# Mixer of a hybrid layer: decay on ScalarE alone, the group norm's factor in steps of their own, and three smaller moves

## The chip, the core and the metric

One core of a Trainium2 chip runs the whole layer in one launch. The metric is device time in microseconds (us), the median of several runs. The engines are TensorE (PE in the rows; PEld its weight loads), VectorE (DVE), ScalarE (ACT), GpSimd (POOL) and SyncE (SP), which issues most loads. Each works through its own queue of instructions in order and waits on semaphores of the others.

## The reference

One decoder layer with 512 tokens of width 1024 in float32: a SwiGLU feed-forward network (FFN1), a mixer, a second one (FFN2), a gated embedding and a final norm. The change touches the mixer alone. Cut to what matters there:

```python
n = rmsnorm(h, mix_norm)
u, v, z, xbc, dt_raw = split(n @ w_in)
ya = rmsnorm(chunked_spatial_gating(gelu(u), gelu(v), ...), gm_out_norm)
xs, b, c = split(silu(causal_depthwise_conv(xbc)))
dt = softplus(dt_raw + dt_bias); a = -exp(a_log)
a_cs = cumsum(dt * a)                               # in chunks of 128 tokens
decay = exp(a_cs[l] - a_cs[s]) for s <= l, else 0   # per head and chunk
y = ((c b^T) * decay) @ (xs * dt) + c @ previous_states * exp(a_cs) + xs * d_skip
y = y * silu(z)
y = y * rsqrt(mean over each of 2 groups (y*y) + eps) * norm_g
h = h + concat(ya, y) @ w_out
```

There are 16 heads of 64 in two groups, a state of 128, and four chunks of 128 tokens.

## The kernel before

Activations lie with features on the 128 partitions and 512 tokens along a row, eight tiles to 1024 features. A float32 product is made of three matmul passes over a high and a low part (L215, L216, L217: high by high, high by low, low by high). A weight tile of 128x1024 is loaded by SyncE (`raw`), cast to its high part on ScalarE (`whi`, L185), and its low part is the difference, made on VectorE (`wlo`, L186); each of the three has three buffers. In a z unit the third matmul is the first that reads `wlo`.

The feed-forward stages stand in an order written out by hand. The mixer's does not: a scheduler places its instructions by the order of the code, by its model of costs and by when buffers come free, and each engine's queue is the result.

The mixer begins with the product for dt (L943 to L954; eight tiles of the normed input, each with a high and a low part), the B and C convolutions and eight convolution tiles `xs`. Then comes the **scan loop** over eight pairs of heads j. A round has these steps:

- `project(13 + j)`, the z unit, 24 matmuls of 512 columns;
- for group 1, states (L1076, L1081, L1082) and `by_token` (transposes L1063, xdt L1065 on VectorE, its scaled copy L1069 on POOL);
- `rows_of`: for the pair after next, ScalarE issues DMAs that spread a head's cumulative sum from DRAM over all partitions (L1091), and in `decayed` two for the grown row (L1109);
- `decayed`: per head, POOL subtracts the column of sums (L1101), VectorE takes the minimum with zero (L1104), ScalarE the exponential (L1105), VectorE multiplies by the masked c b^T (L1106);
- `ssd`: 16 mask products (L1122) and the state products (L1127) on TensorE, then L1131 and L1132 on VectorE and L1133 on POOL add them to y;
- `gated`: z times r/2 (L1141), tanh (L1142), L1143, and y times that on POOL (L1144), whose square goes into the sum of its group's norm (L263 for a group's first tile, L266 and L267 for the next three).

Group 0 is done after pair 3, group 1 after pair 7. The group norm's factor needs four sums over partitions on TensorE (L276), a root in eleven tiny VectorE steps (L233 to L238), a tile of diagonals (L295), a product that spreads it over all partitions (L306), and a copy to SBUF (L312). `finish_group` then multiplies four y tiles (L1150) and splits each in a high part on ScalarE (L199) and a low part on POOL (L200). In the code of before the sums and root of group 0 are called at the first of the eight units of the w_v product, the other steps at the third; group 1's at the fourth and at the sixth.

After w_v come the gating (`mix`, between the u units, with sums for a norm in `gn`, whose additions L267 run on POOL) and the output product, which reads the split y.

Of the kernel before, what the change touches and what calls it, by code (L numbers as in the profile page):

```python
# [26 lines left out]
AF = mybir.ActivationFunctionType  # L27
ALU = mybir.AluOpType

P = 128  # L30
T = 512
NC = T // P
D = 1024
ND = D // P
# [7 lines left out]
D_ORDER = tuple(d + i for d in range(NP) for i in (0, NP))  # L42
# [21 lines left out]
GROUPS = 2  # L64
# [19 lines left out]
def layer_kernel(ctx: ExitStack, tc: tile.TileContext, a: dict, out: bass.AP):  # L84
    nc = tc.nc
# [73 lines left out]
    ps = sm_ps()  # L159
# [11 lines left out]
    class Unit:  # L171
# [11 lines left out]
        def split(self, c0, c1):  # L183
            c = slice(c0, c1)
            nc.scalar.copy(self.hi[:, c], self.raw[:, c])  # L185
            nc.vector.tensor_tensor(  # L186
                self.lo[:, c], self.raw[:, c], self.hi[:, c].bitcast(F32), ALU.subtract
            )
# [759 lines left out]
        both[:, :, :HEADS].bitcast(F32), ALU.subtract,  # L948
    )
    ps = mm_ps()  # L950
    for k in range(ND):
        for i in range(2):
            nc.tensor.matmul(
                ps, both[:, k, :], x[k][i], start=k + i == 0, stop=k + i == ND  # L954
            )
    dt_raw = tmp()
    nc.vector.tensor_copy(dt_raw[: 2 * HEADS], ps[: 2 * HEADS])
# [16 lines left out]
    def chunk(t, c):  # L974
        return t[:, c * P : (c + 1) * P]
# [17 lines left out]
    def hc(t):  # L993
        return t.rearrange("p (h c) -> p h c", c=NC)
# [100 lines left out]
    def decayed(j, ms):  # L1095

        g = j // 4
        for i, m in enumerate(ms):
            hd = 2 * j + i
            m3 = m.rearrange("p (c l) -> p c l", c=NC)  # L1100
            nc.gpsimd.tensor_tensor(  # L1101
                m3, m3, hc(acs)[:, hd, :].unsqueeze(2).to_broadcast([P, NC, P]), ALU.subtract
            )
            nc.vector.tensor_scalar(m, m, 0.0, None, ALU.min)  # L1104
            nc.scalar.activation(m, m, AF.Exp)  # L1105
            nc.vector.tensor_tensor(m, m, cb[g], ALU.mult)  # L1106
        grow = sb("u")
        for i in range(2):
            nc.scalar.dma_start(  # L1109
                grow[i * HD : (i + 1) * HD, :],  # L1110
                cs_dram[1, 2 * j + i : 2 * j + i + 1, :].partition_broadcast(HD),
            )
        return ms, grow
# [30 lines left out]
        nc.gpsimd.tensor_tensor(xs[j], xs[j], z, ALU.mult)  # L1144
        group_norm[j // 4].add(xs[j])

    def finish_group(g, tok):
        rg = Norm.on_all(tok)
        for j in range(4 * g, 4 * g + 4):
            nc.vector.scalar_tensor_tensor(  # L1150
                xs[j], xs[j], col("ssm_norm", j), rg, ALU.mult, ALU.mult
            )
            yb.append(split(xs[j], "yb"))

    xs = []
    for i in range(ND):
# [51 lines left out]
    for half in range(2):  # L1208
        ps = [mm_ps() for _ in range(NC)]
        for u in range(4):  # L1210
            whi, wlo = weights(w_v[half, u], 1024)
            if half == 0:
                if u == 0:
                    group_tok = [group_norm[0].per_token(D // GROUPS)]
                elif u == 2:
                    finish_group(0, group_tok[0])
                elif u == 3:
                    group_tok.append(group_norm[1].per_token(D // GROUPS))
            elif u == 1:
                finish_group(1, group_tok[1])  # L1220
            for c in range(NC):
                for i in range(2):
                    k = 2 * u + i
                    xhi, xlo = (chunk(t, c) for t in x[k])
                    w = slice(i * T, (i + 1) * T)
                    passes(ps[c], xhi, xlo, whi[:, w], wlo[:, w], k == 0, k == ND - 1)
        for c in range(NC):
            t = sb("ya")
            nc.scalar.activation(t, ps[c], AF.Gelu, scale=rtok[:, c : c + 1])
            v[c][half] = t  # L1230
# [33 lines left out]
        bias.append(b)  # L1264

    u = []
    gn = Norm()

    def mix(i):
        ps = sm_ps()  # L1270
# [277 lines left out]
```

## Time and profile before

| | us |
|---|---|
| median of 3 runs | 1109.0 |
| the runs | 1108.41, 1109.0, 1111.56 |
| the profiled execution, its own time | 1109.82 |
| its span in the trace | 1108.1 |
| TensorE busy | 1083.0 |
| VectorE busy | 792.1 |
| ScalarE busy | 494.5 |
| POOL busy | 172.6 |

The profiled execution is one of the program's; its span runs from its first to its last instruction, and 1.7 us lie around it. Its mean granted TensorE clock is 0.996 of full speed. The mixer's scan loop lies at about 445 to 518, the w_v product and the gating behind it. A row of the profile names the line, the engine, the operation and its tiles (output <- inputs) with their shapes. Where a row has a part in square brackets, that is how long the engine sat idle before it and what ended the wait.

### The profile page before, as it was taken

The page shows a single profiled execution, that of the slowest core. Times are in us where ns is not written, and L with a number is a line of the kernel's source. Part 1 is how long each engine was busy: PE and PEld are TensorE (multiplying, and loading weights), DVE is VectorE, ACT ScalarE, POOL GpSimd, SP SyncE. Part 2 cuts the span into 40 slices and gives each one's busy share as a digit, 9 for nine tenths or more (in the row PEclk, how much of TensorE's full clock was granted, in tenths as well). Part 3 has the DMA queues.
Part 4 walks back from the last instruction along what each step waited for, and adds up shares of the span by engine and source line. Part 5 has one row for each costly group of instructions (what it writes and reads, how often), then busy time and mean ns, then how long its engine had stood idle before and what let it go on. Part 6 is the DMA issues. An engine that isn't in the chain of part 4 may idle for free.

```text
span 1108.1 us, 16431 instructions
## 1 busy us (share of the span) xinstructions
PE 1083.0 (98%) x6631; PEld 952.7 (86%) x6631; DVE 792.1 (71%) x1072; ACT 494.5 (45%) x645; POOL 172.6 (16%) x155
## 2 busy tenths in 40 slices
PE   9889999999999999999999999999999999999997
PEld 6779999999998787777788888889999999999887
DVE  5887776766667688898775565768767766667766
ACT  6545444444345374433433343544444443434554
POOL 2001000000001201585421100000000000000311
PEclk9999999999999999999999999999999999999998
DMA  9767756566631223343422233477666666543412
GB/s 352 202 172 198 198 151 183 170 188 159 182 95 57 96 79 107 112 143 116 133 76 95 77 96 114 156 167 196 185 190 190 176 186 176 165 121 110 140 52 77
DMA packets 49036, 161.66 MB, mean 146 GB/s; under 512 B 5568, under 2 KB 5824, under 8 KB 48960
## 3 DMA queue, kind: packets, MB, share of 16 engines
q1 hardware_dynamic: 34128, 117.46, 30.9%
q0 software_dynamic: 9232, 33.56, 16.8%
q10 hardware_dynamic: 5600, 9.60, 2.8%
q8 instruction: 52, 0.85, 0.3%
q14 instruction: 24, 0.20, 0.1%
HBM read 156.33 MB, written 4.26 MB: 145 GB/s over the span
## 4 chain that ended last, share of the span: by engine, by line
PE 77%; DVE 12%; ACT 4%; issue 3%; POOL 2%; DMA 1%; SPq 0%; DVEq 0%; ACTq 0%; POOLq 0%
PE mm L598 18%; PE acc L598 14%; PE sm L216 8%; PE sm L217 8%; PE sm L215 8%; PE mm L215 4%; PE mm L216 4%; PE mm L217 4%; PE acc L215 3%; PE acc L216 3%; PE acc L217 3%; ACT whi L421 1%; DVE wlo L186 1%; DVE wlo L422 1%; DMA u<-cs_dram 1%
## 5 line engine op out<-in xcount | busy, mean ns | idle before, releaser
L598 PE MATMUL mm<-xfb,whi 128*128 128x256 f32 x960 | 166.4, 276 | 0.5 <-ACT whi L421 0.5
L422 DVE TENSOR_TENSOR wlo<-raw,whi 128x1024 fp32r<-128x1024 f32 x93 | 113.9, 1225 | 56.6 <-ACT whi L421 54.6
L598 PEld LDWEIGHTS mm<-xfb,whi 128*128 128x128 f32 x960 | 146.0, 188 | 2.3 <-ACT whi L421 0.7
L598 PE MATMUL mm<-xfb,wlo 128*128 128x256 f32 x480 | 132.8, 277 | 0.8 <-DVE wlo L422 0.8
L421 ACT CAST whi<-raw 128x1024 fp32r<-128x1024 f32 x93 | 97.3, 1047 | 78.4 <-issue 39.2
L217 PE MATMUL sm<-ghi,wlox 128*128 128x512 f32 x296 | 116.3, 393 | 0.0
L216 PE MATMUL sm<-glo,whix 128*128 128x512 f32 x296 | 115.8, 391 | 0.0
L215 PE MATMUL sm<-ghi,whix 128*128 128x512 f32 x296 | 115.2, 389 | 0.0
L598 PE MATMUL acc<-xfb,whi 128*128 128x256 f32 x640 | 111.2, 276 | 0.8 <-DVE g L730 0.8
L598 PEld LDWEIGHTS acc<-xfb,whi 128*128 128x128 f32 x640 | 97.8, 188 | 2.9 <-issue 1.4
L598 PE MATMUL acc<-xfb,wlo 128*128 128x256 f32 x320 | 88.7, 277 | 2.6 <-DVE wlo L422 2.6
L598 PEld LDWEIGHTS mm<-xfb,wlo 128*128 128x128 f32 x480 | 90.1, 188 | 1.0 <-DVE wlo L422 1.0
L422 DVE TENSOR_TENSOR wlox<-rawd,whix 128x1024 fp32r<-128x1024 f32 (+1 forms) x40 | 45.7, 1142 | 58.1 <-ACT whix L421 58.1
L422 DVE TENSOR_TENSOR wlo<-rawb,whi 128x1024 fp32r<-128x1024 f32 x52 | 63.6, 1223 | 21.3 <-ACT whi L421 21.3
L613 POOL DMA_DIRECT2D raw<-in_ffn_gu x20 | 17.3, 863 | 388.1 <-DVE h L790 121.2
L736 ACT ACTIVATE g<-g 128x512 f32<-128x512 f32 x40 | 25.3, 632 | 110.8 <-DVE g L735 110.8
L185 ACT CAST whi<-raw 128x1024 fp32r<-128x1024 f32 x44 | 45.7, 1043 | 59.7 <-PE mm L216 22.7
L186 DVE TENSOR_TENSOR wlo<-raw,whi 128x1024 fp32r<-128x1024 f32 x44 | 57.5, 1308 | 19.5 <-ACT whi L185 14.4
L790 DVE SCALAR_TENSOR_TENSOR h<-sm,h 128x512 f32<-128x512 f32 x96 | 63.5, 685 | 10.9 <-PE sm L217 10.3
L421 ACT CAST whi<-rawb 128x1024 fp32r<-128x1024 f32 x52 | 54.2, 1043 | 26.4 <-DVE rawb L608 19.7
L217 PEld LDWEIGHTS sm<-ghi,wlox 128*128 128x128 f32 x296 | 55.5, 188 | 11.7
L215 PEld LDWEIGHTS sm<-ghi,whix 128*128 128x128 f32 x296 | 55.6, 188 | 11.1 <-DVE h L790 0.4
(393 smaller groups left out, 2657.4 us busy)
## 6 DMA issues: line engine op xcount, KB each, us to landing
raw<-in_ffn_gu SPq DMA_DIRECT2D x56, 512.0 KB, 5.9
rawd<-in_ffn_down SPq DMA_DIRECT2D x40, 512.0 KB, 3.9
rawb<-in_ffn_gu SPq DMA_DIRECT2D x32, 512.0 KB, 5.1
raw<-in_ffn_gu POOLq DMA_DIRECT2D x30, 512.0 KB, 5.5
raw<-in_w_in SPq DMA_DIRECT2D x29, 512.0 KB, 3.6
s<-in_ffn_gu SPq DMA_DIRECT2D x20, 512.0 KB, 7.0
s<-in_ffn_gu POOLq DMA_DIRECT2D x20, 512.0 KB, 8.2
raw<-in_w_out SPq DMA_DIRECT2D x16, 512.0 KB, 3.5
```

The lines of the kernel that those rows point to most:

```text
L185: nc.scalar.copy(self.hi[:, c], self.raw[:, c])
L186: nc.vector.tensor_tensor(self.lo[:, c], self.raw[:, c], self.hi[:, c].bitcast(F32), ALU.subtract)
L215: nc.tensor.matmul(ps, whi, xhi, start=first, stop=False)
L216: nc.tensor.matmul(ps, whi, xlo, start=False, stop=False)
L217: nc.tensor.matmul(ps, wlo, xhi, start=False, stop=last)
L421: nc.scalar.copy(self.hi[:, :n], raw[:, :n])
L422: nc.vector.tensor_tensor(self.lo[:, :n], raw[:, :n], self.hi[:, :n].bitcast(F32), ALU.subtract)
L598: nc.tensor.matmul(o, wt[:, c], xt, start=fresh and p == m == n == 0, stop=last and n == 2, skip_group_check=True,)
L613: nc.gpsimd.dma_start(w21.raw, self.src[0], accum_op=ALU.add)
L736: nc.scalar.activation(t, t, AF.Silu)
L790: nc.vector.scalar_tensor_tensor(h[d], ps[d], 0.5, h[d], ALU.mult, ALU.add)
```

## The change

Five edits in the mixer. In `decayed`, POOL's subtraction and VectorE's minimum go. ScalarE makes four Relu instructions of 128x128 per head, one per chunk, each max(column - row, 0) with the column as bias, and the exponential is taken of minus that, so that the result is the same. The steps of the group norm's factor are functions of their own, called at separate units of w_v. The low parts of y, the split's difference, are made on VectorE, no longer on POOL. The gating norm `gn` adds its squares on VectorE. The product for dt takes its tiles in the order 0, 4, 1, 5, 2, 6, 3, 7 (`D_ORDER`), no longer 0 to 7; that is the order in which FFN1 finishes them.

```diff
--- before.py
+++ after.py
@@ -948,10 +948,10 @@
         both[:, :, :HEADS].bitcast(F32), ALU.subtract,
     )
     ps = mm_ps()
-    for k in range(ND):
+    for n, k in enumerate(D_ORDER):
         for i in range(2):
             nc.tensor.matmul(
-                ps, both[:, k, :], x[k][i], start=k + i == 0, stop=k + i == ND
+                ps, both[:, k, :], x[k][i], start=n + i == 0, stop=n + i == ND
             )
     dt_raw = tmp()
     nc.vector.tensor_copy(dt_raw[: 2 * HEADS], ps[: 2 * HEADS])
@@ -1097,12 +1097,12 @@
         g = j // 4
         for i, m in enumerate(ms):
             hd = 2 * j + i
-            m3 = m.rearrange("p (c l) -> p c l", c=NC)
-            nc.gpsimd.tensor_tensor(
-                m3, m3, hc(acs)[:, hd, :].unsqueeze(2).to_broadcast([P, NC, P]), ALU.subtract
-            )
-            nc.vector.tensor_scalar(m, m, 0.0, None, ALU.min)
-            nc.scalar.activation(m, m, AF.Exp)
+
+            for c in range(NC):
+                nc.scalar.activation(
+                    chunk(m, c), chunk(m, c), AF.Relu, scale=-1.0, bias=hc(acs)[:, hd, c : c + 1]
+                )
+            nc.scalar.activation(m, m, AF.Exp, scale=-1.0)
             nc.vector.tensor_tensor(m, m, cb[g], ALU.mult)
         grow = sb("u")
         for i in range(2):
@@ -1144,13 +1144,25 @@
         nc.gpsimd.tensor_tensor(xs[j], xs[j], z, ALU.mult)
         group_norm[j // 4].add(xs[j])
 
-    def finish_group(g, tok):
-        rg = Norm.on_all(tok)
+
+    group = [{}, {}]
+
+    def group_sums(g):
+        group[g]["ps"] = group_norm[g].sums()
+
+    def group_diagonals(g):
+        group[g]["diags"] = Norm.diagonals(Norm.of_sums(group[g]["ps"], D // GROUPS))
+
+    def group_spread(g):
+        group[g]["ps"] = Norm.spread(group[g]["diags"], group[g]["ps"])
+
+    def finish_group(g):
+        rg = Norm.kept(group[g]["ps"])
         for j in range(4 * g, 4 * g + 4):
             nc.vector.scalar_tensor_tensor(
                 xs[j], xs[j], col("ssm_norm", j), rg, ALU.mult, ALU.mult
             )
-            yb.append(split(xs[j], "yb"))
+            yb.append(split(xs[j], "yb", nc.vector))
 
     xs = []
     for i in range(ND):
@@ -1209,15 +1221,13 @@
         ps = [mm_ps() for _ in range(NC)]
         for u in range(4):
             whi, wlo = weights(w_v[half, u], 1024)
-            if half == 0:
-                if u == 0:
-                    group_tok = [group_norm[0].per_token(D // GROUPS)]
-                elif u == 2:
-                    finish_group(0, group_tok[0])
-                elif u == 3:
-                    group_tok.append(group_norm[1].per_token(D // GROUPS))
-            elif u == 1:
-                finish_group(1, group_tok[1])
+            for fn in {
+                (0, 0): (lambda: group_sums(0),), (0, 1): (lambda: group_diagonals(0),),
+                (0, 2): (lambda: group_spread(0),), (0, 3): (lambda: finish_group(0), lambda: group_sums(1)),
+                (1, 0): (lambda: group_diagonals(1),), (1, 1): (lambda: group_spread(1),),
+                (1, 2): (lambda: finish_group(1),),
+            }.get((half, u), ()):
+                fn()
             for c in range(NC):
                 for i in range(2):
                     k = 2 * u + i
@@ -1264,7 +1274,7 @@
         bias.append(b)
 
     u = []
-    gn = Norm()
+    gn = Norm(nc.vector)
 
     def mix(i):
         ps = sm_ps()
```

The scheduler places the instructions anew; behind the second edited line the line numbers are shifted (L1150 becomes L1162). Three places follow, as the queue of one engine in a row; the numbers behind the names count buffers, and what an instruction waits for stands in brackets.

VectorE, around the low part of z unit 6. First before, where `wlo_4725` is that low part, L1131 to L1132 the sums of pair 4, L1104 the minima of the masks of pair 6:

```order
L1141 SCALAR_TENSOR_TENSOR tmp_4690<-acc_4628,rall_3725 128x512 [waits DVE_49,PE_49]
L1131 SCALAR_TENSOR_TENSOR xs_4098<-xs_4098,vec_70,mm_4674 128x512 [waits PE_49]
L1132 TENSOR_TENSOR u_4596<-u_4596,sm_4675 128x384 [waits DMAHW5_49,DMAHW3_49,PE_49]
L1143 SCALAR_TENSOR_TENSOR tmp_4690<-tmp_4691,tmp_4690 128x512 [waits Activation_49]
L186 TENSOR_TENSOR wlo_4725<-raw_4723,whi_4724 128x1024
L1104 TENSOR_SCALAR u_4670<-u_4670 128x512 [waits DMAHW2_49,Pool_49]
L1104 TENSOR_SCALAR u_4672<-u_4672 128x512 [waits DMAHW3_49,Pool_49]
L1106 TENSOR_TENSOR u_4670<-u_4670,ya_4062 128x512 [waits Activation_49]
```

Then the same place after, where `wlo_4749` is that low part and L1131, L1132 the sums of pair 5:

```order
L1141 SCALAR_TENSOR_TENSOR tmp_4788<-acc_4722,rall_3725 128x512 [waits PE_49,Pool_49]
L1143 SCALAR_TENSOR_TENSOR tmp_4714<-tmp_4715,tmp_4714 128x512 [waits Activation_49]
L1131 SCALAR_TENSOR_TENSOR xs_4147<-xs_4147,vec_70,mm_4772 128x512 [waits PE_49]
L186 TENSOR_TENSOR wlo_4749<-raw_4747,whi_4748 128x1024 [waits DMAHW5_49,Activation_49]
L1132 TENSOR_TENSOR u_4691<-u_4691,sm_4773 128x384 [waits DMAHW1_49,DMAHW0_49]
L1106 TENSOR_TENSOR u_4694<-u_4694,ya_4062 128x512 [waits Activation_49]
L1106 TENSOR_TENSOR u_4696<-u_4696,ya_4062 128x512 [waits Activation_49]
```

The low part stood behind L1143 and now stands behind L1131 of the pair just ahead of the unit, and that waits for TensorE; the minima are gone from the row.

ScalarE, one round of the decay. First before, where `u_4516` and `u_4518` are the masks of one pair, L1109 and L1091 issue row copies:

```order
L1091 DMA u_4516<-cs_dram 128x512 [waits DMAHW1_49,PE_49]
L1091 DMA u_4518<-cs_dram 128x512 [waits DMAHW2_49,PE_49]
L1109 DMA u_4596<-cs_dram 64x512 [waits DMAHW3_49,PE_49]
L266 ACTIVATE tmp_4542<-xs_3985 128x512 [waits Activation_49,Pool_49]
L1109 DMA u_4596<-cs_dram 64x512 [waits DMAHW5_49]
L1091 DMA u_4599<-cs_dram 128x512 [waits DMAHW6_49,DVE_49]
L1091 DMA u_4601<-cs_dram 128x512 [waits DMAHW7_49,PE_49]
L1105 ACTIVATE u_4516<-u_4516 128x512 [waits DVE_49]
L1105 ACTIVATE u_4518<-u_4518 128x512 [waits DVE_49]
L1142 ACTIVATE tmp_4620<-tmp_4619 128x512
L1109 DMA u_4667<-cs_dram 64x512 [waits DMAHW0_49,PE_49]
L1109 DMA u_4667<-cs_dram 64x512 [waits DMAHW1_49]
```

Then after, where `u_4694` and `u_4696` are the rows of a pair, first issued and then read by Relu (L1102), and L185 is the cast of a z unit's weights:

```order
L1102 ACTIVATE u_4621<-u_4621,acs_3944 128x128 x3
L1109 DMA u_4691<-cs_dram 64x512 [waits PE_49]
L1105 ACTIVATE u_4621<-u_4621 128x512 [waits Activation_49]
L1109 DMA u_4691<-cs_dram 64x512
L1091 DMA u_4694<-cs_dram 128x512 [waits DMAHW2_49,PE_49]
L1091 DMA u_4696<-cs_dram 128x512 [waits DMAHW7_49,DMAHW3_49]
L1142 ACTIVATE tmp_4715<-tmp_4714 128x512 [waits DVE_49]
L185 CAST whi_4748<-raw_4747 128x1024
L1102 ACTIVATE u_4694<-u_4694,acs_3944 128x128 [waits DMAHW2_49]
L1102 ACTIVATE u_4694<-u_4694,acs_3944 128x128
L263 ACTIVATE ssum_4720<-xs_4098 128x512 [waits Pool_49]
L1102 ACTIVATE u_4694<-u_4694,acs_3944 128x128 x2
```

The exponential waited for VectorE's minimum; now a Relu waits for the DMA of its row, with one tanh and one cast between the DMA's issue and it, and the squares (L263) stand among the Relus.

VectorE, the diagonals of group 0 (L295), ahead of the first tile of y that is multiplied by the factor. First before, where L236 to L238 are the end of the root:

```order
L236 TENSOR_TENSOR nt_4904<-ny_4903 128x4 [waits DVE_49]
L237 SCALAR_TENSOR_TENSOR nt_4904<-nt_4904,nv_4902 128x4 [waits DVE_49]
L238 SCALAR_TENSOR_TENSOR rtok_4901<-nt_4904,ny_4903 128x4 [waits DVE_49]
L295 TENSOR_TENSOR tmp_4976<-ident_72,rtok_4901 128x512 [waits DVE_49,Pool_49]
L186 TENSOR_TENSOR wlo_5028<-raw_5026,whi_5027 128x1024 [waits DMAHW4_49,Activation_49]
L186 TENSOR_TENSOR wlo_5090<-raw_5088,whi_5089 128x1024 [waits DMAHW5_49,Activation_49]
L1150 SCALAR_TENSOR_TENSOR xs_3895<-xs_3895,vec_70,rall_4980 128x512 [waits Activation_49]
```

Then after, where `wlo_4959` to `wlo_5106` are low parts of w_v's units and L1141, L1143 the gate of the last pair:

```order
L1141 SCALAR_TENSOR_TENSOR tmp_4909<-mm_4868,rall_3725 128x512 [waits DVE_49,Pool_49]
L186 TENSOR_TENSOR wlo_4959<-raw_4957,whi_4958 128x1024 [waits DMAHW4_49,Activation_49]
L1143 SCALAR_TENSOR_TENSOR tmp_4909<-tmp_4910,tmp_4909 128x512 [waits Activation_49]
L186 TENSOR_TENSOR wlo_5006<-raw_5004,whi_5005 128x1024 [waits DMAHW1_49]
L295 TENSOR_TENSOR tmp_4978<-ident_72,rtok_4963 128x512 [waits DVE_49,Pool_49]
L186 TENSOR_TENSOR wlo_5037<-raw_5035,whi_5036 128x1024 [waits DMAHW4_49,Activation_49]
L186 TENSOR_TENSOR wlo_5106<-raw_5104,whi_5105 128x1024 [waits DMAHW5_49,Activation_49]
L1162 SCALAR_TENSOR_TENSOR xs_3895<-xs_3895,vec_70,rall_5041 128x512 [waits Activation_49]
```

The root's steps have left this place: they now stand ahead of the last pair's L1143, between the mask multiplications of the last pair. The diagonals stand between low parts of w_v's units. On TensorE the spread (L306) keeps its place, the same number of instructions from the start, while the sums of group 0 now stand ahead of z unit 7.

## Rows read from the trace of the kernel before

**Rows 1.** Page, part 1: busy us, share and instructions of each engine.

```profile
PE 1083.0 (98%) x6631; PEld 952.7 (86%) x6631; DVE 792.1 (71%) x1072; ACT 494.5 (45%) x645; POOL 172.6 (16%) x155
```

**Rows 2.** Whom TensorE waited for: us in total, times, longest.

```profile
PE mm L1122 <- DVE u L1106: 2.4, 3, 1.3
PE sm L306 <- DVE tmp L295: 2.3, 1, 2.3
PE mm L217 <- DVE wlo L186: 1.7, 1, 1.7
...
PE mm L953 <- DVE convin L961: 0.7, 1, 0.7
...
PE sm L276 <- POOL ssum L267: 0.3, 1, 0.3
```

**Rows 3.** Windows: length, busy PE, PEld, DVE, ACT, POOL; granted clock, DMA share, GB/s.

```profile
444.80:518.30 73.50, 69.38 (x393) 55.66 (x392) 66.83 (x79) 29.82 (x42) 47.80 (x34) 1.00 0.42 128
518.30:530.00 11.70, 11.70 (x58) 9.73 (x56) 8.27 (x16) 2.87 (x5) 6.74 (x6) 1.00 0.29 91
530.00:536.00 6.00, 3.71 (x9) 2.09 (x8) 5.22 (x9) 2.34 (x3) 1.22 (x1) 0.72 0.19 61
```

**Rows 4.** Timeline of TensorE at the spread: start, length, instruction, idle time before.

```profile
529.67 0.39 PE L216 MATMUL mm<-wlo,x 128*128 128x512 f32 x1
529.90 0.39 PE L217 MATMUL mm<-whi,x 128*128 128x512 f32 x1
532.58 2.04 PE L306 MATMUL sm<-tmp,ones 128*128 128x512 f32 x2 [2.29 <-DVE tmp L295]
...
535.70 0.45 PE L215 MATMUL mm<-whi,x 128*128 128x512 f32 x1
```

**Rows 5.** POOL's groups, 430 to 740: busy us, mean ns, idle before.

```profile
L1101 POOL TENSOR_TENSOR u<-u,acs 128x512 f32<-128x512 f32 x16 | 21.0, 1320 | 7.2 <-DMA u<-cs_dram 7.2
...
L1144 POOL TENSOR_TENSOR xs<-xs,tmp 128x512 f32<-128x512 f32 x8 | 13.6, 1698 | 3.2 <-DVE tmp L1143 2.8
...
L1069 POOL TENSOR_TENSOR u<-yb,toend 128x512 f32<-128x512 f32 x5 | 7.1, 1429 | 16.2 <-DVE yb L1065 16.2
```

**Rows 6.** VectorE's groups, 430 to 540, in the same columns.

```profile
L1104 DVE TENSOR_SCALAR u<-u 128x512 f32<-128x512 f32 x16 | 14.5, 923 | 0.9 <-POOL u L1101 0.9
...
L1143 DVE SCALAR_TENSOR_TENSOR tmp<-tmp,tmp 128x512 f32<-128x512 f32 x8 | 5.8, 727 | 0.0
...
L1131 DVE SCALAR_TENSOR_TENSOR xs<-xs,vec,mm 128x512 f32<-128x512 f32 x4 | 3.0, 739 | 0.0
```

**Rows 7.** Timeline of VectorE and POOL: two low parts, one beside POOL.

```profile
461.74 1.22 DVE L186 TENSOR_TENSOR wlo<-raw,whi 128x1024 fp32r<-128x1024 f32 x1
...
467.99 1.39 POOL L1133 TENSOR_TENSOR xs<-xs,u 128x384 f32<-128x384 f32 x1 [2.69 <-DVE u L1132]
...
468.43 2.03 DVE L186 TENSOR_TENSOR wlo<-raw,whi 128x1024 fp32r<-128x1024 f32 x1
```

**Rows 8.** ScalarE's groups with a column as operand, two widths.

```profile
L1374 ACT ACTIVATE tmp<-tmp,vec 128x512 f32<-128x512 f32 x5 | 3.6, 714 | 0.4 <-DVE tmp L1373 0.3
...
L1374 ACT ACTIVATE tmp<-tmp,vec 128x256 f32<-128x256 f32 x6 | 3.0, 496 | 2.1 <-DVE tmp L1373 2.1
```

**Rows 9.** Timeline of ScalarE: two instructions behind each other.

```profile
464.12 0.63 ACT L263 ACTIVATE ssum<-xs 128x512 f32<-128x512 f32 x1 [0.68 <-POOL xs L1144]
464.66 0.61 ACT L1105 ACTIVATE u<-u 128x512 f32<-128x512 f32 x1
```

**Rows 10.** Line L1091, the masks' row copies: from issue to landing.

```profile
DMA to landing us min/median/max: 3.0/3.5/5.2
```

**Rows 11.** Line L1109, row copies: ns per issue, min/median/max; first and last start.

```profile
L1109 ACTq DMA_DIRECT2D u<-cs_dram x16: 452/453/1456, 442.3 to 508.5; - x16
```

**Rows 12.** Timeline of TensorE: mask products of two pairs, five pairs apart.

```profile
461.72 1.58 PE L1122 MATMUL acc<-u,yb 128*64 128x128 f32 x16
...
507.78 1.58 PE L1122 MATMUL acc<-u,yb 128*64 128x128 f32 x16
```

## The prediction

> **What bounds the kernel now.** I read the busy times first: TensorE is busy 1083 of 1108 us [rows 1], so only its idle time, some 25 us, and a fallen clock can be won, and of these only what lies in the mixer. The list of who TensorE waited for [rows 2] names the places that the change can touch: the decay masks (L1122 behind L1106, 2.4 us in 3 waits), the spread of group 0's factor (L306 behind L295, 2.3), the low part of one z unit (L217 behind L186, 1.7), the last tile of dt's product (L953, 0.7) and the sums of a norm (L276 behind POOL's L267, 0.3). Then by stage [rows 3]: from the first z product to the end of the scan loop (444.8 to 518.3) TensorE is busy 69.4 of 73.5, idle 4.1; VectorE is busy 66.8 there, ScalarE 29.8, POOL 47.8. Around the spread (530 to 536) TensorE is busy 3.7 of 6.0 at a granted clock of 0.72. The single rows show it [rows 4]: the last matmul starts at 529.90, the spread at 532.58, and the matmuls after it come 0.43 apart up to 535.70, where full speed has them 0.23 apart (529.67 to 529.90).
>
> **The change part by part.**
>
> *The old waits of the scan loop, -4.1.* Per pair of heads two POOL subtractions (1.32 us each) and two VectorE minima (0.92) go: 16 x 1.32 = 21.0 us off POOL and 14.5 off VectorE [rows 5, 6]. VectorE also gets faster where POOL was running: a wlo subtraction takes 1.22 when POOL is still, and 2.03 when it starts 0.44 into a POOL instruction of 1.39 [rows 7], so VectorE is held until POOL has ended. With 66.8 - 14.5 = 52 us of work in 73.5, VectorE no longer trails the loop, and I drop all 4.1 us of the old idle time. Only the 0.5 of L1076 just ahead of 444.8 stays.
>
> *The work that ScalarE gets, hidden.* 64 Relu instructions of 128x128 with a column as bias are in no row. The same form takes 0.714 at 512 columns and 0.496 at 256 [rows 8]; the line through both gives 0.39 at 128, and since the next instruction starts about 0.09 before the end of one (464.12 to 464.66 for 0.63) [rows 9], 0.30 per step: 64 x 0.30 = 19 us. Bounds: a quarter of the 512 price, 0.18 (11 us), and the 256 price less the overlap, 0.41 (26 us). I take the line, as 128 lies nearest the 256 row on it. ScalarE would be busy 49 of 73.5 us. What is new is its queue order: the copies that bring pair j+2's rows are issued, then come one tanh, one weight cast and at once the Relus that wait for these copies. They land 3.5 us after issue (3.0 to 5.2) [rows 10]; behind the waiting Relus stand the next tanh and the next whi cast. A round is 3.5 landing + 8 x 0.30 Relu + 0.54 square + two exponentials 1.2 + three issues of 0.45 [rows 11] = 9.0 us. TensorE needs 46.1 us for five pairs (461.72 to 507.78) [rows 12], 9.2 each, and the masks are made a pair ahead. So I cost it at nothing; what decides this is in the third rival.
>
> [...]
>
> *New waits in the loop, +6.6.* The order on VectorE puts wlo of a z unit directly behind L1131 of the pair before it, and L1131 waits for that pair's last mask matmul on TensorE. TensorE goes straight on to the z unit, whose third matmul needs wlo. Chain: L1131, 0.74 long, next start 0.66 on [rows 6], wlo 1.22 free or 2.03 behind POOL [rows 7], hand-offs 0.1: 2.0 to 2.8. Two matmuls cover 0.23 + 0.39 = 0.6 [rows 4]. So 1.4 to 2.2 idle.
> - z unit 2: L1143 just ahead starts POOL's L1144, so nearly the upper end, 2.15.
> - z unit 6: L1143 runs while VectorE waits for TensorE, so half of POOL's time is over, 1.7.
> - z unit 7: group 0's sums now stand between, about 0.95 of small matmuls: 0.45 to 1.25, I take 0.7.
> - z unit 5: the pulled-up state products of later pairs cover it, 0.1.
> - z unit 3: a state product now stands after its second matmul and waits for L1069, which POOL does after L1144. From the transposes L1143 0.6, L1144 1.7, L1069 1.4 [rows 5, 6] with a start half a step late: 4.2, covered by the pair's products 2.3 and two matmuls 0.45: 1.5 (0.2 with POOL's fastest runs, 2.0 if also L1082 comes late).
> - pair 1, second head: L1132 now stands ahead of its L1106 and waits for that pair's state products; 0.5 + 0.7 less the first head's 0.8: 0.5 (0 to 1).
> Sum 6.6, between 3.5 and 8.7. Units 2 and 6 come near the one idle stretch (2.3) after which the clock fell; 1.7 (unit 6 of before) left it alone. I take no fall, and keep 1.6 for one in the range.
>
> *Group norm's factor, -3.9.* The spread keeps its place among TensorE's products; only VectorE's order moves. Group 0's sums come a z unit earlier, and the eleven tiny steps of the root and the diagonals no longer stand behind L1143 of the last pair; the diagonals stand behind the wlo of w_v's third unit, which is needed by the same matmuls anyway. By the rows, TensorE reaches the spread at about 530 [rows 4], while wlo is made some 4 us earlier. So 2.3 of waiting goes [rows 2] and with it the stretch at the lower level: 3.2 us of work at half speed, 1.6. If the fall has another cause, 2.3.
>
> *Low parts of y on VectorE, 0.* Eight subtractions (0.68 each, 5.4 us) come to VectorE, which has 3.4 us free in the 11.7 from 518.3 [rows 3], and more behind; they are read by products 80 us later. *Gating norm's sums, -0.3:* seven additions of 0.68 on VectorE in place of POOL; the last stands behind the last square, and TensorE's 0.3 wait goes [rows 2]. *dt's tiles, 0:* tiles finish as 0, 4, 1, 5, 2, 6, 3, 7, and the last in either order is tile 7; the one wait of the product (0.7) [rows 2] is for its last matmul.
>
> Sum: -4.1 + 6.6 - 3.9 - 0.3 = -1.7. The profiled execution took 1109.8, so 1108.1 by it; it lies 0.8 above the median of 1109.0, so I forecast 1107.3. With the bounds of the new waits 1104.2 to 1109.4, with a fall of the clock 1111.
>
> **The rivals.**
>
> *The new waits don't come or are half as long* (the lower ends, 3.5 us and less). For it: VectorE has 21 us of POOL's work less to be held by, so that it may reach L1131 with POOL still. Against: L1144 is started by the instruction two rows ahead. Down to none: 1109.0 - 4.1 - 3.9 - 0.3 = 1100.7; at 2 us of waits 1102.7, which I name as its time. [...]
>
> *Group norm's wait stays:* the diagonals stand behind a wlo that waits for a load and a cast; if that cast comes after 530, nothing of the 3.9 is won: 1107.3 + 3.9 = 1111.2. That part would then not do what it says. Against it: w_v loads are issued over 10 us ahead.
>
> *ScalarE's round becomes the bound, slower.* The round decides from about 9.6 us: 9.2 per pair plus 0.4 for the waits above. With 0.41 a Relu step (+0.9) and copies that land at 4.35 (+0.85), halfway between median and maximum, it is 10.7, and six rounds cost 6 x 1.1 = 6.6: 1107.3 + 6.6 = 1114. For it: 64 instructions in no row, and the casts of the z units queue behind. Against: the copies were 3.5 at the median under the same traffic.
>
> **How the numbers follow.** 0.3%, 3.3 us, is about what a measurement of this kernel can tell from no change: faster is below 1105.7, slower above 1112.3. Forecast 0.50 (of it 0.12 below 1105.7, 0.02 above 1112.3 with two falls of the clock), shorter waits 0.25, group norm's wait stays 0.11, ScalarE's round 0.14. Faster 0.12 + 0.25 = 0.37; slower 0.02 + 0.14 = 0.16; same 0.47. The range of 8 in 10 is 1101.5 to 1112: it leaves out ScalarE's case and the end of the shorter waits' case.
>
> **What would show it.** In the changed kernel's list of waits, L306 behind L295 gone and the clock at 1.0 from 530 to 536; TensorE's L217 behind L186 in two or three z units at 1.4 to 2.2, and L1076 behind POOL; no wait of L1122 over 0.5; Relu rows at 0.39; ScalarE's idle time ahead of Relus put down to the row copies, some 2 us a round. The forecast is wrong if L217 never waits, if the idle sum of the loop is under 3 us, or if L1122 waits for exponentials in the last pairs.

## The result, and the profile after

The changed kernel took 1112.15 us at the median of 14 runs (1109.2 to 1113.08), the kernel before 1109.22 (14 runs, 1107.98 to 1111.7): a ratio of 1.0020 with a 95% interval of 1.0012 to 1.0028, so 2.2 us slower (1.3 to 3.1). A second set, run later, gave 1111.23 against 1109.59, 1.0014 (1.0004 to 1.0024). Forecast were 1107.3, in a range from 1101.5 to 1112.0. The profiled execution took 1111.42 with a span of 1109.7, 1.6 more than before; in the second set's trace the span is 1109.2.

The page's part 1 of the changed kernel, beside [rows 1]:

```profile
PE 1085.0 (98%) x6631; PEld 954.1 (86%) x6631; DVE 781.7 (70%) x1071; ACT 513.8 (46%) x709; POOL 132.0 (12%) x124
```

POOL lost 40.6 us and VectorE 10.4, ScalarE gained 19.3. TensorE executes as many matmuls as before, yet is busy 2.0 us longer: that is a sign of the clock, as a matmul at the lower level is busy for longer (0.62 at 468.27 against 0.40 at 464.67 in the timeline below). TensorE's idle time is 24.7 us, 0.4 less than before. Then whom TensorE waited for in the changed kernel (us in total, times, longest), the rows that answer to [rows 2]:

```profile
PE mm L217 <- DVE wlo L186: 4.2, 3, 1.9
...
PE sm L1076 <- POOL u L1069: 2.1, 2, 1.5
...
PE mm L953 <- DVE convin L961: 0.8, 1, 0.8
...
PE acc L1122 <- DVE u L1106: 0.3, 1, 0.3
```

The masks' 2.4 fell to 0.3, and the spread's 2.3 (L306 behind L295) and the 0.3 of L276 behind POOL are in the list no more. In their place stand 4.2 behind wlo and a new wait of 1.5 at L1076, whose 0.5 of before stayed. The windows (length, busy PE, PEld, DVE, ACT, POOL, granted clock, DMA share, GB/s), the first and the last row of stretches like those of [rows 3], the two between them the places where the clock was low:

```profile
444.80:519.00 74.20, 68.25 (x368) 53.71 (x367) 47.50 (x61) 46.28 (x103) 27.67 (x19) 0.95 0.36 111
...
468.20:471.70 3.50, 3.50 (x11) 2.72 (x10) 2.09 (x3) 2.48 (x7) 1.10 (x1) 0.51 0.71 236
509.20:512.70 3.50, 3.50 (x10) 2.72 (x10) 1.59 (x2) 2.45 (x6) 0.35 (x1) 0.51 0.81 235
530.00:536.60 6.60, 6.60 (x30) 5.30 (x29) 4.94 (x4) 1.78 (x3) 3.51 (x3) 1.00 0.55 159
```

Around the spread the clock is 1.00 and TensorE has no gap, where [rows 3] had 3.71 busy of 6.00 at 0.72. But within the loop there are now two stretches of 3.5 us at 0.51 of full speed. The timeline of TensorE and VectorE shows where the first comes from (start, length, instruction, idle time before):

```profile
464.44 0.75 DVE L1131 SCALAR_TENSOR_TENSOR xs<-xs,vec,acc 128x512 f32<-128x512 f32 x1
...
464.67 0.40 PE L216 MATMUL mm<-x,whi 128*128 128x512 f32 x1
...
465.11 1.85 DVE L186 TENSOR_TENSOR wlo<-raw,whi 128x1024 fp32r<-128x1024 f32 x1
...
467.01 0.50 PE L217 MATMUL mm<-x,wlo 128*128 128x512 f32 x1 [1.95 <-DVE wlo L186]
...
468.27 0.62 PE L216 MATMUL mm<-x,whi 128*128 128x512 f32 x1
468.69 0.63 PE L217 MATMUL mm<-x,wlo 128*128 128x512 f32 x1
...
508.00 0.50 PE L217 MATMUL mm<-x,wlo 128*128 128x512 f32 x1 [1.78 <-DVE wlo L186]
```

In z unit 2, L1131 starts when the pair's last mask product is done, wlo follows and takes 1.85, the third matmul waits 1.95 us, and 1.3 us after it starts the matmuls stand 0.42 apart instead of 0.23. Eight of them cost 8 x 0.2 = 1.6 us. Unit 6 has the same after its 1.78 us. The second trace of this kernel shows both waits (4.1 in 3, the longest 1.9) and both stretches at the same places (granted clock 0.995, in the first 0.994).

The granted clock is on record for every run of the changed kernel, and for the 85 runs of the kernel before that were made beside the experiments. By clock, the number of runs and their mean span (us):

| granted clock | before | changed |
|---|---|---|
| 0.998 | 32 runs, 1106.6 | none |
| 0.997 | 8 runs, 1107.9 | none |
| 0.996 | 26 runs, 1108.2 | 3 runs, 1107.7 |
| 0.995 | 15 runs, 1109.2 | 5 runs, 1109.3 |
| 0.994 | 4 runs, 1109.7 | 13 runs, 1110.3 |
| 0.993, 0.992 | none | 4 runs, 1110.5 |

At the same clock the two kernels take the same time within 0.6 us. The changed kernel is slower because it runs at a lower clock more often.

### The profile page after: what moved, and what is told of

It reads as the page before. It is cut to its first block, busy times and chain, and to the rows that moved or that the text cites. A ratio compares the mean times of both kernels' runs of the same rounds, so it can differ in the third digit from the quotient of the medians.

```text
span 1109.7 us, 16404 instructions
## 1 busy us (share of the span) xinstructions
PE 1085.0 (98%) x6631; PEld 954.1 (86%) x6631; DVE 781.7 (70%) x1071; ACT 513.8 (46%) x709; POOL 132.0 (12%) x124
## 4 chain that ended last, share of the span: by engine, by line
PE 83%; DVE 9%; ACT 4%; issue 2%; POOL 1%; DMA 1%; SPq 0%; DVEq 0%; ACTq 0%; POOLq 0%
PE mm L598 18%; PE acc L598 14%; PE sm L216 8%; PE sm L217 8%; PE sm L215 7%; PE mm L217 5%; PE mm L215 5%; PE mm L216 5%; PE acc L215 3%; PE acc L217 3%; PE acc L216 3%; DVE wlo L186 1%; ACT whi L421 1%; DVE wlo L422 1%; PE sm L1282 1%
## 5 line engine op out<-in xcount | busy, mean ns | idle before, releaser
L185 ACT CAST whi<-raw 128x1024 fp32r<-128x1024 f32 x44 | 45.8, 1043 | 61.3 <-PE mm L216 22.6
L217 PE MATMUL mm<-x,wlo 128*128 128x512 f32 x160 | 64.6, 404 | 4.2 <-DVE wlo L186 4.2
```

Source lines behind the costliest of these rows:

```text
L217: nc.tensor.matmul(ps, wlo, xhi, start=False, stop=last)
```

## The experiments

Theory A came from the two traces: the waits moved as forecast, and what turned the gain into a loss are the two falls of the clock behind the new waits, 3.2 us. The rivals are named where they are tested. The expectations put the waits some 0.2 above the rows (2.1 and 1.9 for 1.95 and 1.78, 1.7 for 1.51, 1.9 for before's 1.71). All ratios are to the kernel before; line numbers in the rows are shifted where an edit adds lines.

**Which edit does what.** Two kernels with one part each, and one with the other four edits.

```diff
-            m3 = m.rearrange("p (c l) -> p c l", c=NC)
-            nc.gpsimd.tensor_tensor(
...
+            for c in range(NC):
+                nc.scalar.activation(
+                    chunk(m, c), chunk(m, c), AF.Relu, scale=-1.0, bias=hc(acs)[:, hd, c : c + 1]
+                )
...
```

> The kernel before with the decay on ScalarE alone; the four other edits are left out. Theory A (the decay moves everything that moved): in this kernel TensorE's order from the scan loop to group 0's spread is that of the changed kernel, group 0's sums ahead of z unit 7 included, and so the waits behind wlo (2.1, 1.9 and 0.6), the wait of L1076 (1.7) and the two stretches at half clock (1.6 each) come, the spread's 3.9 goes: 1111 to 1113, as the changed kernel (1112.2). Rival B (the separate steps of the group norm's factor won the 3.9): the spread waits 2.3 as before and its clock falls: about 1116.

Measured: 1112.52, 1.0021 (1.0013 to 1.0030). Its trace has the changed kernel's waits, and no wait of the spread (between 440 and 540, whole list):

```profile
PE mm L217 <- DVE wlo L186: 4.1, 3, 1.9
PE sm L1076 <- POOL u L1069: 2.0, 2, 1.5
PE acc L1122 <- DVE u L1106: 0.3, 1, 0.3
```

So the decay alone makes the whole difference, and it is also what frees the spread. Rival B falls. The group norm's steps alone, put into the kernel before:

```diff
-                if u == 0:
-                    group_tok = [group_norm[0].per_token(D // GROUPS)]
...
+                (0, 0): (lambda: group_sums(0),), (0, 1): (lambda: group_diagonals(0),),
...
```

> The kernel before with the group norm's factor in steps of their own; the four other edits are left out. Theory A: group 0's sums stay behind the last pair on TensorE and the diagonals keep their place on VectorE behind the last pair's gate, so the spread waits 2.3 as before and the stretch at half clock stays: 1109.2, within 1 us of before. Rival B (the separate steps win the 3.9): 1105.3.

Measured: 1110.32, 1.0005 (0.9995 to 1.0015); the spread waits on, and the clock falls after it as before:

```profile
PE sm L306 <- DVE tmp L295: 2.2, 1, 2.2
```

```profile
530.00:532.60 2.60, 0.39 (x3) 0.06 (x1) 2.39 (x6) 1.81 (x2) 1.28 (x1) 1.00 0.00 0
532.60:536.00 3.40, 3.40 (x7) 1.99 (x8) 3.06 (x4) 0.70 (x2) 0.00 (x0) 0.52 0.40 98
```

The four edits without the decay (the first diff undone in the changed kernel):

> The changed kernel without its decay edit: group norm's steps, y's low parts, gating norm's sums and dt's order stay. Theory A (these four move nothing but the 0.3 at the gating norm's sums): the loop's old waits (4.1), the spread's wait and its half clock stay as before: 1109.2 - 0.3 = 1108.9, within 1 us of before. Rival B (a part of the 2.2 loss or a gain comes from them): off by more than 1.5 us.

Measured: 1109.15, 1.0000 (0.9991 to 1.0009): they are worth nothing that can be told from zero. This trace has the spread's wait of 2.2 too, but no fall of the clock behind it.

**What the falls of the clock cost.** Two extra matmuls in two units, nothing else moved:

```diff
+        if unit - 13 in (2, 6):
...
+            for _ in range(2):
+                nc.tensor.matmul(ps, nought, x[0][0], start=False, stop=False)
```

> The changed kernel with only two more matmuls with a zero weight tile (0.45 us) behind the second matmul of z units 2 and 6; all other instructions keep their places on every engine. The third matmul of these units waits for the same wlo, so its time doesn't move; only the idle time ahead of it falls from 2.1 and 1.9 to 1.7 and 1.5 us. Theory A (the two falls follow from the length of these idle stretches, and 1.7 us of idle time at z unit 3 and 1.9 in the kernel before left the clock alone): no stretch at half clock, 1112.2 - 3.2 = 1109.0, 1108.3 to 1110. Rival D (the falls come from the run of work around, not from these stretches' length): both stay, 1112.2.

Measured: 1108.93, 0.9997 (0.9988 to 1.0005); by the ratios 2.6 us below the changed kernel's first set and 1.9 below its second. The idle time before the third matmul is 0.45 shorter, which is what the two extra ones take, so that it starts no earlier in the unit (2.70 us after the first matmul, 2.68 in the changed kernel), and behind it the clock stays at 1.00 in both units (TensorE's row of unit 2, then two windows):

```profile
467.98 0.50 PE L945 MATMUL mm<-x,wlo 128*128 128x512 f32 x1 [1.50 <-DVE wlo L186]
```

```profile
468.20:474.00 5.80, 5.80 (x25) 4.38 (x25) 3.06 (x4) 4.37 (x10) 2.06 (x2) 1.00 0.58 195
507.00:513.00 6.00, 5.58 (x25) 4.38 (x26) 2.67 (x4) 4.43 (x10) 1.01 (x1) 1.00 0.70 191
```

Two matmuls of no use in each of two units make the kernel faster. Rival D falls. The gain is less than the 3.2 of both falls: in unit 7 wlo now starts beside POOL's gate product and takes 1.93 in place of 1.22, and TensorE waits 1.3 for it there, no longer 0.4. With eight of them in each of the two units, and the state product moved by the scheduler:

> The changed kernel, with eight more matmuls of 512 columns with a zero weight tile (1.8 us) behind the second matmul of z units 2 and 6, where TensorE waits 2.1 and 1.9 for wlo. They add zero to the sum. The scheduler puts the state product of z unit 3 behind that unit, so its wait of 1.7 should go too. Theory A (the clock falls since TensorE stood idle there): idle 0.1 to 0.4 left at both places, no stretch at half clock in the loop: 1112.2 - 3.2 - 1.7 = 1107.3. Rival D (the falls have another cause than these two idle stretches): two stretches of 8 matmuls at 0.43 apart stay: 1110.5.

Measured: 1106.81, 0.9969 (0.9959 to 0.9980), the only version that is clearly faster than both kernels. Its whole list between 440 and 540, and the loop:

```profile
PE sm L1088 <- POOL u L1081: 0.6, 1, 0.6
PE mm L217 <- DVE wlo L186: 0.4, 1, 0.4
PE acc L1134 <- DVE u L1118: 0.3, 1, 0.3
```

```profile
444.80:520.00 75.20, 73.80 (x407) 58.78 (x407) 51.65 (x76) 50.01 (x107) 28.96 (x21) 1.00 0.40 123
```

Of the 73.8 us some 3.7 are the sixteen extra matmuls (16 x 0.23): by that estimate a version without wlo's wait and without them would be worth that much more. The next ones looked for it.

**Taking wlo's wait away.** First by the order of the matmuls in a unit:

```diff
+            for k, (xhi, xlo) in enumerate(x):
+                nc.tensor.matmul(ps, whi[:, k * P : (k + 1) * P], xhi, start=k == 0, stop=False)
+                nc.tensor.matmul(ps, whi[:, k * P : (k + 1) * P], xlo, start=False, stop=False)
+            for k, (xhi, xlo) in enumerate(x):
+                nc.tensor.matmul(ps, wlo[:, k * P : (k + 1) * P], xhi, start=False, stop=k == ND - 1)
```

> The changed kernel, but in the eight z units the 16 matmuls with the high part of the weights come first and the 8 with the low part last, so that 16 matmuls (3.7 us) and no longer 2 (0.6 us) cover the making of wlo. Theory A (the loss is the wait for wlo and the clock that falls after it): waits of 2.1, 1.9 and 0.6 go but for some 1.0 in unit 6 (wlo stands behind L1131, L1132, L1143 and L1141 there) and 0.2 in others, L1076's 1.7 goes since the state product now stands among more matmuls or waits 0.5, the two falls (3.2) go: 1112.2 - 8 = 1104, 1103 to 1106. Rival C (the loss of the loop is ScalarE's round: Relus that wait for row copies): the waits turn up ahead of the mask products instead: 1109 to 1112.

Measured: 1113.66, 1.0031 (1.0019 to 1.0044). Theory A's number was wrong. The wait for wlo in the loop is gone, but others came (masks, then the sums of group 0), and the trace has three falls of the clock, at 504.5 (0.50 from 504.8 to 507.9), 521.6 (eight mask products take 1.97 us from 521.86, 1.09 from 520.32) and 528.5 (0.57 from 528 to 532):

```profile
PE acc L1131 <- DVE u L1115: 2.6, 3, 1.8
...
PE sm L276 <- DVE u L1141: 1.4, 1, 1.4
```

Rival C named the place, not the cause. ScalarE's timeline ahead of the last pair's masks:

```profile
513.29 0.70 ACT L1111 ACTIVATE u<-u,acs 128x128 f32<-128x128 f32 x2 [1.08 <-DMA u<-cs_dram]
...
517.52 0.63 ACT L266 ACTIVATE tmp<-xs 128x512 f32<-128x512 f32 x1 [3.53 <-POOL xs L1153]
518.05 0.97 ACT L1111 ACTIVATE u<-u,acs 128x128 f32<-128x128 f32 x3
...
520.32 1.09 PE L1131 MATMUL acc<-u,yb 128*64 128x128 f32 x8 [1.82 <-DVE u L1115]
```

The row copy of the first head had landed by 513.29, when two of its Relus (L1111 here) ran. The others stand in ScalarE's queue behind a square of the group norm (L266), which waits 3.53 us for POOL's gate product (L1153 here); in the changed kernel the same square waits 1.51. The kernel before has such squares too, but only the two exponentials of a pair share their queue; now eight Relus and two exponentials do.

Then by making the low part in two halves:

```diff
+        for c0, c1 in zip((0,) + tuple(cuts), tuple(cuts) + (n,)):
+            nc.vector.tensor_tensor(
+                w.lo[:, c0:c1], w.raw[:, c0:c1], w.hi[:, c0:c1].bitcast(F32), ALU.subtract
+            )
...
+            w = weights(w_in[14 + j], D, (512,))
```

> The changed kernel, but the low part of each z unit's weights is made by two VectorE instructions of 512 columns in place of one of 1024, so that the third matmul waits for the first half only. Theory A (TensorE waits for VectorE's work behind L1131): the waits of z units 2 and 6 shrink from 2.1 and 1.9 to some 1.4 and 1.3 and that of unit 7 goes (-1.8 together), no fall of the clock (-3.2), the wait of L1076 at unit 3 stays at 1.7 to 2.0: 1112.2 - 5 = 1107.2; with one fall left 1108.8. Rival E (VectorE is held until POOL's instruction ends whatever its own length, so that the first half ends no sooner): 1111 to 1112.5.

Measured: 1108.76, 0.9994 (0.9983 to 1.0005). In unit 6 the wait is 1.25; L1076's wait is gone. In unit 2 it is 2.17 and the clock falls after it (0.59 from 466.0 to 470.2), since there POOL ran two instructions one behind the other and another VectorE instruction stands between L1131 and wlo:

```profile
463.88 1.37 POOL L1137 TENSOR_TENSOR xs<-xs,u 128x384 f32<-128x384 f32 x1 [7.04 <-DVE xs L1135]
464.32 3.17 DVE L195 TENSOR_TENSOR wlo<-raw,whi 128x512 fp32r<-128x512 f32 x2
465.21 1.73 POOL L1148 TENSOR_TENSOR xs<-xs,tmp 128x512 f32<-128x512 f32 x1
465.85 0.50 PE L221 MATMUL mm<-x,wlo 128*128 128x512 f32 x1 [2.17 <-DVE wlo L195]
```

Both theories hold at one unit each: the two halves take 1.76 in unit 6, and 3.17 in unit 2 where POOL is at work from 463.88 to 466.94. Unit 7 still waits 0.8, and behind it the clock falls as well:

```profile
514.50:518.20 3.70, 3.70 (x11) 2.89 (x10) 3.46 (x12) 3.67 (x9) 1.83 (x2) 0.54 0.47 164
```

At the same granted clock this version is below the kernel before: at 0.995 its four runs have a mean span of 1107.0, before's fifteen 1109.2.

Then by moving the gate's product off POOL:

```diff
-        nc.gpsimd.tensor_tensor(xs[j], xs[j], z, ALU.mult)
+        nc.vector.tensor_tensor(xs[j], xs[j], z, ALU.mult)
```

> The changed kernel with the gate's product (L1144) on VectorE in place of POOL. The scheduler then puts wlo of z units 2 and 6 ahead of L1131, and of units 5 and 7 behind L1131 and the gate's product, and the state product of group 1 behind z unit 3. Theory A (what counts is where wlo stands against L1131): no wait at units 2, 3 and 6; at units 5 and 7 L1131 0.74, the product 0.9 and wlo 1.22 less 0.6 of cover: 2.2 each, so two falls again: 1112.2 - 6.2 + 4.4 = 1110.4, and 1107 if neither falls. Rival F (VectorE's load decides): 8 instructions of 0.9 more make VectorE late all through the loop: 1114 or more.

Measured: 1112.12, 1.0027 (1.0017 to 1.0038). The expectation misread the order for unit 2, whose wlo also stands behind L1131 and the gate's product; the waits for wlo there and at unit 7 are the longest of the study, and at unit 6, where wlo stands ahead of L1131 and the sums of group 0 cover it, it is 0.50:

```profile
469.17 0.79 PE L217 MATMUL mm<-x,wlo 128*128 128x512 f32 x1 [2.72 <-DVE wlo L186]
...
518.23 0.50 PE L217 MATMUL mm<-x,wlo 128*128 128x512 f32 x1 [2.88 <-DVE wlo L186]
```

So what stands between the last mask product and wlo decides, as theory A has it. The two falls that it expected are one: the clock is at 0.53 from 468.9 to 472.5, behind unit 2, but at 1.00 from 518.2 to 526, behind the longest wait of all:

```profile
468.90:472.50 3.60, 3.33 (x8) 2.67 (x9) 3.60 (x6) 2.58 (x7) 1.38 (x1) 0.53 0.73 219
518.20:526.00 7.80, 7.77 (x42) 6.06 (x42) 5.76 (x9) 5.36 (x8) 2.53 (x3) 1.00 0.29 89
```

TensorE's other waits in the loop are no longer than in the changed kernel, which speaks against rival F.

Then by making all three parts of the weights one pair earlier, in the changed kernel and in the kernel before:

```diff
-    w = weights(w_in[13], D)
+    ws_z = [weights(w_in[13], D), weights(w_in[14], D)]
     for j in range(ND):
...
+        if j < ND - 2:
+            ws_z.append(weights(w_in[15 + j], D))
+        pz = project(13 + j, ws_z[j])
```

> The changed kernel with the z units' weights loaded, cast and split one pair earlier (two units ahead, with the same three buffers). The scheduler then puts wlo of a unit some twelve VectorE instructions ahead of where it was, and mixes mask products into the middle of the z units. Theory A (the loss is wlo standing behind L1131 and the clock falls after it): no wait for wlo at units 2, 6 and 7 (4.6 gone), none of L1076 (1.7), no fall (3.2), some 1 of new waits for masks: 1112.2 - 8.5 = 1103.7, 1102 to 1106. Rival C (ScalarE's round, with its waits for row copies, is the bound once wlo is out of the way): waits ahead of mask products of 4 and more: 1108 to 1112.

> The kernel before with the z units' weights loaded, cast and split one pair earlier, no other edit; TensorE's order is that of the kernel before. Theory A: only its wait at unit 6 (1.9) can go, the masks' waits (2.9 with the first one's) and the spread's 3.9 stay: 1107.5, 1106.5 to 1109. Against the run of the changed kernel with the same edit this gives what the decay on ScalarE is worth without the wait for wlo: some 4. Rival G (the gain is the earlier weights' and the decay is worth nothing): the two come out within 1 us of each other.

Measured: 1123.6, 1.0128 (1.0111 to 1.0145), and 1109.70, 1.0004 (0.9994 to 1.0013); theory A's numbers missed both. In the kernel before, unit 6's wait goes, the masks' grow from 2.4 to 3.3, and the clock falls behind the longest of them (2.0; the granted clock of the trace is 0.994, of before's 0.996). In the changed one wlo's waits are gone, and it is by far the slowest:

```profile
PE mm L1122 <- DVE u L1106: 6.0, 3, 3.3
PE acc L1122 <- DVE u L1106: 5.4, 2, 5.0
```

That is rival C's place, and again with ScalarE standing in a square (2.87 us for POOL's gate product) ahead of Relus of the pair whose masks TensorE waits 5.0 for. About 1.1 of the 5.0 are VectorE's own: the exponential of the first mask ends at 530.86, and its L1106 starts at 531.92, behind the last step of group 0's root. Rival G falls with the same two numbers: what the earlier weights do depends wholly on the decay, though the other way round than expected. The last run took the squares off ScalarE:

```diff
-        group_norm[j // 4].add(xs[j])
...
+            nc.gpsimd.tensor_tensor(sq, xs[j], xs[j], ALU.mult)
+            nc.gpsimd.tensor_tensor(n.totals[0], n.totals[0], sq, ALU.add)
```

> The kernel of e9 (weights one pair earlier, 1123.6) with the squares of the group norm made on POOL in place of ScalarE; the orders of TensorE and VectorE stay nearly those of e9. In e9 TensorE waits 11.4 us for masks, up to 5.0, and ahead of the late masks ScalarE stands in a square that waits 2.9 us for POOL's gate product, with the Relus of the next pair queued behind it. Theory H (it is the square that holds the Relus, and with them closes a ring from the mask products over y, the gate and the square to the next masks): the masks' waits fall below 4, 1108 to 1113. Rival C (the Relus wait for their row copies, whatever stands ahead): the waits stay above 8, 1119 or more.

Measured: 1119.70, 1.0086 (1.0069 to 1.0102). The masks' waits fell from 11.4 to one of 4.3, near theory H's bound of 4, but the time fell by 3.9 only and missed its range. H is right about what held the Relus; it left out what stands behind it. The rows ahead of the last pair's masks:

```profile
516.44 0.63 ACT L1105 ACTIVATE u<-u 128x512 f32<-128x512 f32 x1
...
522.46 0.16 DVE L233 TENSOR_SCALAR nv<-sm 128x4 f32<-128x4 f32 x1 [1.94 <-PE sm L276]
...
526.00 0.68 DVE L1106 TENSOR_TENSOR u<-u,ya 128x512 f32<-128x512 f32 x1
...
526.74 2.84 PE L1122 MATMUL acc<-u,yb 128*64 128x128 f32 x16 [4.32 <-DVE u L1106]
```

ScalarE is done with that pair at 517.07, 9 us before the mask is multiplied. The wait that is left is in VectorE's queue: the mask's L1106 stands behind the root of group 0, whose first step (L233) waits for the sums on TensorE. No run moved the root, so this is read from the rows and not tried by itself. It is also not most of e12's 10 us: against before, TensorE is idle 2.5 us longer in the trace (27.6 for 25.1) and busy 7.4 longer, and the clock falls four times ahead of the last 20 us (0.91 on the mean from 460 to 480, 0.83 from 520 to 540, 0.992 over the trace), where before's trace has one fall (0.94 from 520 to 550, 0.996).

**A second trace of the changed kernel**, unchanged:

> The changed kernel once more, for a second trace. The two traces' spans differ by 1.6 us, the medians by 2.9. Theory A: the waits are the same to 0.2, and what differs from execution to execution is where the clock falls: a stretch at half clock more (1.4 to 1.6) at about 38 us, in FFN1, as in other traces of this study. 1112.2 within 0.6.

Measured: 1111.23. The waits are 4.1 and 2.0, as in the first trace, with both falls in the loop. The fall at 38 us, in FFN1, is not in this trace, and not in the first either (1.00 from 0 to 40 us), so it is not what separates them. It is in the traces of e1, e4, e5, e7, e8, e9, e10 and e12, kernels on both sides of before; e4's and e5's clock is 1.00 from 444.8 to 520 and 0.996 over the trace.

## Why the prediction was wrong, point by point

- **Old waits of the loop, -4.1: right.** L1122 behind L1106 went from 2.4 to the 0.3 that is counted below, and the 1.7 of before's unit 6 has given way to the wait at unit 6 below.
- **New waits, +6.6: right in size and place.** Listed are 4.2 behind wlo, 1.5 at L1076 and 0.3 at the second head, 6.0 in sum; 1.95 at unit 2 (forecast 2.15), 1.51 at unit 3 (1.5), 1.78 at unit 6 (1.7), 0.4 at unit 7 (0.7), none at unit 5 (0.1), 0.3 at the second head (0.5).
- **"I take no fall": this is the step that failed.** The forecast's sum is a change of -0.1 in idle time (-4.1 + 6.6 - 2.3 - 0.3) and of -1.6 in busy time, the fall at the spread. In the traces idle time changed by -0.4 and busy time by +2.0. Two falls at 1.6 each are 3.2 us, and -1.7 + 3.2 = +1.5, which is within both measured intervals and near the 1.6 of the spans. e5 shows it: without the two falls the kernel is back at before (0.9997). It is not at -1.7, which lies outside e5's interval (-1.3 to +0.6); 0.9 of the difference is the longer wait at unit 7, the other 0.5 is within the interval. The prediction had one row of a fall (2.3 us idle) and one without (1.7), forecast waits of 2.15 and 1.7, and put both on the side without, though 2.15 is nearer to 2.3. In the changed kernel the clock fell behind 1.78 as well, so that these two rows could not have told. It priced the case of two falls, and gave it 0.02.
- **Group norm's factor, -3.9: right in size for the trace it was read from, wrong in cause.** e2 shows that the separate steps leave the 2.2 us wait, e1 that the decay alone removes it: without the decay's subtractions and minima (35.5 us) the scheduler puts group 0's sums ahead of z unit 7 (517.27 in e1, 518.36 and behind the last mask products in e2). That the 2.3 went all the same was luck. The 1.6 for the fall is not there in every execution: e7 has the wait and no fall, and 32 of the 85 runs of before have a granted clock of 0.998, above the 0.996 of the trace with this one fall. The rival in which the wait stays had the right doubt on the edit, for another reason.
- **Relu steps: right.** 388 ns each against 0.39, 20.7 us in all against 19, and 7.1 us of waiting, in six waits and not some 2 us in each of eight rounds, for row copies that landed 3.7 us after issue at the median. The row of the decay in the changed kernel:

```profile
L1102 ACT ACTIVATE u<-u,acs 128x128 f32<-128x128 f32 x64 | 20.7, 388 | 7.1 <-DMA u<-cs_dram 7.1
```

  The decay on ScalarE lost time all the same, as e1 alone is at 1.0021, but not by the price of the instructions: they took 20.7 us on ScalarE, 35.5 us left POOL and VectorE, and TensorE's waits for masks fell from 2.4 to 0.3. What cost was the order of VectorE's queue that came with the edit.
- **ScalarE's round as the bound: not in this kernel, but one move away.** Its price left out that a square in the round waits for POOL. In the changed kernel ScalarE waits 22.4 us ahead of its squares, and TensorE 0.3 for masks; in e3 and e9 it is on the path.
- **Low parts of y, gating norm's sums, dt's order: right**, within what e7 can tell. The wait of 0.3 at L276 went.

The medians of the first set lie 2.9 apart and the spans of the two profiled executions 1.6, since the executions of one kernel lie 3.7 us apart (before) and 3.9 (changed), and go with the granted clock: before's profiled run, at 0.996, took 0.6 more than its median (40 of the 85 runs were at 0.997 or 0.998), the changed kernel's 0.7 less. Open is why one execution has a fall that another of the same kernel lacks.

## What to carry to other kernels

Where TensorE is the bound (98% busy here), count new waits one by one: here they came to 6.0 us in sum, and behind those of 1.95 and 1.78 came 3.5 us each at 0.51, some 1.6 us more. Price each that comes near an idle stretch with a fall in the trace as if the clock fell. Two matmuls of no use in each of two such waits took 2.6 us off the changed kernel (1.9 by the second set), where the edit had cost 2.2. Where two kernels lie this close, compare their runs at the same granted clock. An engine that is given a step's work in its queue also gives that step all the waits of what stands ahead of it there, as e3's Relus had a square's 3.53 us for POOL: list what each instruction ahead waits for, not only how long it runs.

## What the runs showed of the hardware

- Falls of the clock came behind idle stretches, but not by their length alone. In the changed kernel it fell behind 1.95 and 1.78 us and not behind 1.51; it did not behind the 1.71 of before's unit 6 and the 1.50 of e5, but did behind the 0.8 of e6's unit 7; in e8 it stayed at 1.00 behind 2.88, the longest wait for wlo in any run; in e7 the spread waited 2.2 us, as in e2, and the clock behind it stayed at 1.00:

```profile
533.70:539.00 5.30, 5.30 (x22) 4.04 (x23) 5.30 (x7) 1.94 (x4) 0.00 (x0) 1.00 0.51 179
```

- The fall need not come at once: after the spread of e2 the first matmuls were slow already (0.52 from 532.60 on), in the changed kernel's loop 1.3 us of work at full speed came first (467.01 to 468.27, 508.00 to 509.27). The window rows of low clock above are 3.4 to 3.7 us long, at 0.51 to 0.54; in e9 one fall lasted 6.8 (0.83 on the mean from 520 to 540).
- A subtraction on VectorE from and to SBUF of 128x1024 took 1.21 to 1.23 us where POOL was still at its start and 1.47 to 2.30 where POOL was at work first (before, 430 to 555); each of these five, which started at 468.43, 473.22, 482.33, 500.50 and 523.74, ended 1.08 or 1.09 us after POOL's instruction. In the changed kernel one started at 487.40, 0.23 ahead of a POOL instruction: it took 1.22, and POOL's 2.13 in place of 1.27. In e6 two of half the size took 3.17 together beside two POOL instructions.
